# Keys and values of both layers by seven half-size products instead of eight

## The chip, the cores and the metric

The kernel runs on one core of a Trainium2 chip. The metric is the device time in microseconds of one execution, the median of several runs; lower is better. The core has a matrix engine (TensorE, PE in the profile; its weight loads are PEld), VectorE (DVE), ScalarE (ACT), GpSimd (POOL) and SyncE (SP). DMAs are issued from the SP queue and from the POOL queue.

## The reference, cut to what matters

Two layers work on 512 tokens of width 1024. Each layer is, with `mod` six vectors made from `c` by one product:

```
h = rmsnorm(x, norm1_w) * (1 + sc1) + sh1
u = h @ w_in          # pool 256, conv 3 x 256, q 512, k 512, v 512, gates 3 x 1024
q, k: RMS norm over each head of 64, partial rotary;  o = block-sparse causal attention(q, k, v)
merged = sig(g0)*(y_pool @ p_pool) + sig(g1)*(y_conv @ p_conv) + sig(g2)*(o @ p_attn)
x = x + g1 * (merged @ w_out)
h2 = rmsnorm(x, norm2_w) * (1 + sc2) + sh2
x = x + g2 * ((silu(h2 @ w_gate) * (h2 @ w_up)) @ w_down)
```

## The kernel before, in words

All activations stand with features on the 128 partitions and the 512 tokens along a row, eight tiles `k` for the width of 1024. Every product is done as three matmuls (`mm3`, L166): each operand is split into a rounded part `hi` and the rest `lo`, and hi\*hi, hi\*lo and lo\*hi are added in PSUM. One `mm3` of 512 columns adds 512 to a counter, and each 2048 columns (12 matmuls) make one **tick** (L137). A tick advances the running generators ("fibers", which hold attention's own work) and lets queued small tasks (`bulk`) be emitted, as far as a credit that grows by `bulk_rate` per tick covers their listed cost.

Weights come as a list of **chunks** of up to eight 128 x 128 blocks (`items`, L310). `next_w` (L366) hands out the next chunk and loads those up to four (later three) chunks ahead of it. A chunk is fetched by SP into a `raw` tile (three buffers, L235), its hi copy is made by ACT (L328) and its lo part by DVE (L331). Gate columns (`by_transfer`) are split without DVE: ACT makes hi (L339) and its negative (L341), and a POOL DMA adds the weights from memory to the negative (L343). There are five hi and five lo tiles, so a chunk can be split only when the chunk five before it has been used. The tag `w4` has six buffers of 4 KB per partition, `big` has 46 of 2 KB, and PSUM has four banks of tag `mm` and two pairs of tag `pair`.

A layer's first half runs in this order on PE. (1) q and three feature columns, chunk by chunk as the norm delivers tiles `k`. (2) The feature columns 6, 3 and 7 of pool and convolution. (3) `wide()` twice: keys, then values, each as four chunks of eight blocks, 4 token tiles x 8 `k` x 3 matmuls of 512 columns. After the keys, squares and sums for their norm are made (`qk_evac`, L608 to L611), and key scaling and rotary (L989, L626 to L629) are queued. After the values, ACT and DVE split them into `v` (L1003, L1004). (4) Attention starts as a fiber after three ticks, beside columns 4 and 5 with the pool product, then eight steps `j` of two gate columns and four small products into two `mm` banks each (`p1`, `p2`), then six columns of the third gate. (5) `drain()` ends attention; then eight attention products, merged with the gates (L1033, L1067, L573). (6) The output product, the second norm and the feed-forward, whose gate and up products already run as seven half-size products (`glu_pair`).

The products of `c` (`ada_dot`, L399) are made by DVE from loaded rows, one dot of 128 x 1024 per task; `pin` places an instruction behind the one traced before it on its engine. The dots of part G1 are queued beside keys and values; in layer 0 those of SC2 and SH2 are queued beside attention at a `bulk_rate` of 0.27, each dot with its own load just ahead of it (L433).

The compiler that places the instructions keeps each engine's queue in a fixed order, chosen from the program's order and from when it takes operands to be ready; buffers of one tag are handed out in the order asked for.

## Time and profile before

| | us |
|---|---|
| median of 3 runs | 1442.67 (1441.82 to 1442.86) |
| the profiled execution, its own time | 1442.24 |
| its span, first to last instruction | 1440.5 |
| PE busy | 1433.7 |
| DVE busy | 1014.5 |
| ACT busy | 714.0 |
| POOL busy | 145.7 |

The profiled execution's time is 1.7 us over its span, for what lies around it. Busy time is the union of an engine's instructions. Matmuls overlap (one is shown as 390 ns but the next starts 227 ns later), so PE's pace is read from starts, not from durations. Layer 0's stages (2), (3) and the start of (4) lie at 55.6, 72.0 and 115.5 us; layer 1's at 763.5, 781.8 and 825.4 us.

### The profile page before, as it was taken

How to read it: one execution, taken by the hardware profiler on the slowest of the kernel's cores; microseconds unless marked ns; L12 is line 12 of the kernel's file. 1: busy time of each engine (PE TensorE's matmuls, PEld its weight loads, DVE VectorE, ACT ScalarE, POOL GpSimd, SP SyncE). 2: the span in 40 equal slices, each digit the busy share in tenths (PEclk: the TensorE clock that was granted, in tenths of full speed). 3: DMA queues.
4: the chain of work that ended last, by engine and by line, in shares of the span. 5: the costliest groups of instructions: out<-in, count | busy, mean ns of one | idle time of the engine just before them, and what ended most of it. 6: DMA issues, size and time to landing. Idle time of an engine off the chain costs nothing.

```text
span 1440.5 us, 21954 instructions
## 1 busy us (share of the span) xinstructions
PE 1433.7 (100%) x8346; PEld 1261.7 (88%) x8346; DVE 1014.5 (70%) x1858; ACT 714.0 (50%) x1199; POOL 145.7 (10%) x204
## 2 busy tenths in 40 slices
PE   9999999999999999999999999999999999999999
PEld 7888888888988998999988888888889989999997
DVE  8887777649686867677798766654578747657663
ACT  5645666733653452535444466666336625525450
POOL 0000110101100311210000000011020102111200
PEclk9999999999999999999999999999999999999999
DMA  9647876665347766756536565567372537637532
GB/s 351 216 149 209 220 184 168 181 229 163 90 140 223 187 179 206 190 146 198 189 125 207 177 146 135 135 154 194 129 208 85 136 114 180 173 105 187 136 88 85
DMA packets 91049, 241.83 MB, mean 168 GB/s; under 512 B 11576, under 2 KB 24256, under 8 KB 90944
## 3 DMA queue, kind: packets, MB, share of 16 engines
q1 hardware_dynamic: 67312, 177.37, 36.8%
q0 software_dynamic: 23040, 62.93, 22.3%
q8 instruction: 65, 1.06, 0.3%
q14 instruction: 40, 0.33, 0.1%
q10 hardware_dynamic: 592, 0.14, 0.0%
HBM read 238.30 MB, written 2.10 MB: 167 GB/s over the span
## 4 chain that ended last, share of the span: by engine, by line
PE 96%; issue 1%; DMA 1%; DVE 1%; ACT 0%; ACTq 0%; DVEq 0%; POOLq 0%
PE mm L151 83%; PE pair L151 12%; PE mm L157 1%; DMA wlo<-in_ws 1%; DMA colt<-in_cols 0%; DVE big L788 0%; DVE big L795 0%; DVE big L562 0%; ACT whi L339 0%; DVE w L399 0%; ACT big L1028 0%; DVE wlo L331 0%; ACT big L575 0%; DVE tmp L555 0%; ACT big L559 0%
## 5 line engine op out<-in xcount | busy, mean ns | idle before, releaser
L151 PE MATMUL mm<-big,whi 128*128 128x512 f32 (+1 forms) x4350 | 1078.0, 339 | 1.0 <-ACT big L1028 1.0
L151 PEld LDWEIGHTS mm<-big,whi 128*128 128x128 f32 x4350 | 744.3, 190 | 87.8 <-issue 2.6
L151 PE MATMUL mm<-big,wlo 128*128 128x512 f32 (+1 forms) x2175 | 735.3, 338 | 0.1
L151 PEld LDWEIGHTS mm<-big,wlo 128*128 128x128 f32 x2175 | 412.6, 190 | 45.3 <-DMA wlo<-in_ws 0.5
L328 ACT ACTIVATE whi<-raw 128x1024 fp32r<-128x1024 f32 (+2 forms) x192 | 198.2, 1034 | 223.2 <-PE mm L151 116.8
L331 DVE TENSOR_TENSOR wlo<-raw,whi 128x1024 fp32r<-128x1024 f32 (+2 forms) x192 | 225.8, 1187 | 53.1 <-ACT whi L328 52.6
L328 ACT ACTIVATE whi<-w 128x1024 fp32r<-128x1024 f32 x72 | 76.2, 1058 | 139.5 <-PE mm L151 85.8
L1073 DVE SCALAR_TENSOR_TENSOR x<-mm,mod,x 128x512 f32<-128x512 f32 (+1 forms) x89 | 61.6, 694 | 75.2 <-PE mm L151 75.0
L399 DVE SCALAR_TENSOR_TENSOR w<-w,csil 128x1024 f32<-128x1024 f32 x80 | 95.9, 1221 | 17.8 <-DMA w<-in_ada 17.7
L331 DVE TENSOR_TENSOR wlo<-w,whi 128x1024 fp32r<-128x1024 f32 x72 | 86.8, 1221 | 28.8 <-ACT whi L328 28.1
L257 POOL DMA_DIRECT2D w<-in_ws x72 | 47.2, 673 | 465.1 <-DVE wlo L331 214.4
L343 POOL DMA_DIRECT2D wlo<-in_ws x48 | 41.0, 855 | 438.1 <-ACT wlo L341 241.5
L259 POOL DMA_DIRECT2D w<-in_ws x72 | 63.4, 906 | 159.0 <-DMA w<-in_ws 155.3
L151 PE MATMUL pair<-whi,big 128*128 128x512 f32 x224 | 76.7, 389 | 0.0
L339 ACT ACTIVATE whi<-raw 128x1024 fp32r<-128x1024 f32 x48 | 51.0, 1063 | 49.4 <-PE mm L151 32.1
L151 PE MATMUL pair<-big,whi 128*128 128x256 f32 (+1 forms) x376 | 74.0, 294 | 0.0
L151 PEld LDWEIGHTS pair<-big,whi 128*128 128x128 f32 x376 | 60.4, 191 | 2.2
L151 PE MATMUL mm<-whi,big 128*128 128x512 f32 x160 | 56.9, 392 | 0.6 <-ACT big L559 0.4
L1033 DVE SCALAR_TENSOR_TENSOR big<-big,mm 128x512 f32<-128x512 f32 x48 | 32.8, 684 | 33.1 <-PE mm L151 31.8
L151 PE MATMUL pair<-big,wlo 128*128 128x256 f32 (+1 forms) x188 | 55.3, 294 | 0.0
L341 ACT ACTIVATE wlo<-whi 128x1024 fp32r<-128x1024 f32 x48 | 50.8, 1059 | 0.3
L151 PEld LDWEIGHTS pair<-whi,big 128*128 128x128 f32 x224 | 42.1, 188 | 8.6
(212 smaller groups left out, 1349.3 us busy)
## 6 DMA issues: line engine op xcount, KB each, us to landing
raw<-in_ws SPq DMA_DIRECT2D x146, 512.0 KB, 4.4
w<-in_ada SPq DMA_DIRECT2D x80, 512.0 KB, 5.5
w<-in_ws POOLq DMA_DIRECT2D x144, 256.0 KB, 4.7
wlo<-in_ws POOLq DMA_DIRECT2D x48, 512.0 KB, 6.8
raw<-in_ws SPq DMA_DIRECT2D x64, 256.0 KB, 4.1
raw<-in_ws SPq DMA_DIRECT2D x24, 384.0 KB, 3.6
raw<-in_ada SPq DMA_DIRECT2D x16, 512.0 KB, 4.4
raw<-in_ws SPq DMA_DIRECT2D x16, 448.0 KB, 5.5
```

The lines of the kernel that those rows point to most:

```text
L151: tc.keep_in_program_order(T.matmul(*a, **k))
L157: tc.keep_in_program_order(T.transpose(*a))
L257: nc.gpsimd.dma_start(dst, self.source(0, 1))
L259: nc.gpsimd.dma_start(dst, self.source(*other), accum_op=ALU.add)
L328: A.activation(hi[:, :n], raw[:, :n], AF.Copy)
L331: ins = V.tensor_sub(lo[:, :n], raw[:, :n], f32(hi)[:, :n])
L339: A.activation(hi[:, :n], raw[:, :n], AF.Copy)
L341: A.activation(lo[:, :n], f32(hi)[:, :n], AF.Copy, scale=-1.0)
L343: nc.gpsimd.dma_start(lo[:, i:i + m].rearrange("p b n -> p (b n)"), src, accum_op=ALU.add)
L399: return V.scalar_tensor_tensor(aw, aw, 1.0, csil, op0=ALU.mult, op1=ALU.mult, accum_out=mod[l][:, part, j:j + 1])
L1033: V.scalar_tensor_tensor(sg, sg, 1.0, branch, op0=ALU.add, op1=ALU.mult)
L1073: V.scalar_tensor_tensor(x[k][:, lo:hi], src, mod[l][:, part, k:k + 1], x[k][:, lo:hi], op0=ALU.mult, op1=ALU.add)
```

## The change

Keys and values are now one product of a 2 x 2 block matrix: tokens 0 to 255 and 256 to 511 against the two halves of the width, and the two halves of the width against keys and values. It is done by seven block products (forms) instead of eight. The sums on the activation side are made by DVE (`sums_one`, `sums_two`) from a full f32 copy `h` of the normed activations, which ACT now writes in the first norms too. The sums on the weight side are made partly by POOL DMAs that add (`summed`), partly by DVE (`tensor_add` on `x`). Each form takes two chunks, so there are fourteen chunks in place of eight, each used by 12 matmuls instead of 24. Partial results are read out of PSUM between forms by ACT and DVE. The order of forms is B21, B11, R1, -V, B22, T3, T4.

Behind keys and values come three gate columns (20, 28, 21), then columns 4 and 5, then gate 29. Attention starts after five ticks instead of three. Pool weights, both convolution chains and the second pool chain are queued after keys and values instead of before. The rotary tables of layer 0 are made within them. The G1 dots move behind `drain()`, at a rate of 1.3; SC2 and SH2 run from step `j` = 2 at 0.5, each load one dot ahead.

```diff
+KEYS = 12
+AFTER_KEYS = (20, 28, 21, 4, 5, 29)
+    class KeyValue:
+        SUBS = 14
+        def blocks(self, kk, z, cp):
+            return [("in", kk * HK + 2 * cp + i, KEYS + 4 * z + b) for i in range(2) for b in range(4)]
+        def summed(self, tile, other, cp):
+            flat = tile.rearrange("p b n -> p (b n)")
+            nc.gpsimd.dma_start(flat, self.source(0, 1, cp))
+            nc.gpsimd.dma_start(flat, self.source(other[0], other[1], cp), accum_op=ALU.add)
+        def load(self, sub):
+            form, cp = divmod(sub, 2)
+            if sub == 0:
+                self.x = [w4([P, C_BLOCKS, P]) for _ in range(2)]
+                for i in range(2):
+                    self.summed(self.x[i], (1, 1), i)
+            if form == 0:
+                return split_w(self.raw(1, 0, cp), C_BLOCKS)
+            if form == 1:
+                self.near[cp] = self.raw(0, 0, cp)
+                return split_w(self.near[cp], C_BLOCKS)
+            if form == 2:
+                w = split_w(self.x[cp], C_BLOCKS)
+                pin(V.tensor_add(self.x[cp], self.x[cp], self.near[cp]))
+                self.near[cp] = self.raw(1, 0, cp)
+                return w
+            if form == 3:
+                w = split_w(self.x[cp], C_BLOCKS)
+                pin(V.tensor_add(self.x[cp], self.x[cp], self.near[cp]))
+                self.far[cp] = rawt()
+                self.summed(self.far[cp], (0, 0), cp)
+                return w
+            if form == 4:
+                return split_w(self.x[cp], C_BLOCKS)
+            return split_w(self.far[cp] if form == 5 else self.raw(1, 1, cp), C_BLOCKS)
...
         def step(n):
+            if early and n + 1 < len(every):
+                load(n + 1)
...
-            if i == 1:
-                A.activation(self.h[k][:, lo:hi], t[:, lo:hi], AF.Identity, bias=sh)
+            A.activation(self.h[k][:, lo:hi], t[:, lo:hi], AF.Identity, bias=sh)
...
+            A.activation(self.h[k], self.t, AF.Identity, bias=mod[0][:, SH1, k:k + 1])
...
-        def wide():
...
+        def sums_one(c):
+            V.tensor_sub(t3, h2[:, BLOCK:], h1[:, BLOCK:])
+            V.tensor_sub(r1, h1[:, :BLOCK], h1[:, BLOCK:])
+            V.scalar_tensor_tensor(nv, t3, -1.0, h1[:, :BLOCK], op0=ALU.mult, op1=ALU.subtract)
+            return one, two, split_from(one)
+        def sums_two(c, one, two):
+            V.scalar_tensor_tensor(two[:, BLOCK:], one[:, BLOCK:], -1.0, norm.h[HK + c][:, :BLOCK],
+                                   op0=ALU.mult, op1=ALU.subtract)
+            return split_from(two)
+        def keys_values(qk, ss, made, tables, then):
+            def form(o, name, start):
+                for cp in range(2):
+                    w = next_w()
+                    for t in range(2):
+                        for i in range(2):
+                            c = 2 * cp + i
+                            mm3(o[t], cut(rows(name, c), slice(None), slice(t * P, (t + 1) * P)), wrow(w, 4 * i),
+                                start and c == 0, c == HK - 1, skip_group_check=not start)
+                    yield cp
+            for _ in form(e, "B21", True):
+            for _ in form(a, "B11", True):
+            for t in range(2):
+                A.activation(qk[t][:, 1], heads(a[t]), AF.Copy)
+                V.tensor_add(qk[t][:, 1], qk[t][:, 1], heads(e[t]))
+                squares(1, ss, t, qk[t][:, 1].rearrange("p h d -> p (h d)"))
+            for cp in form(c, "R1", True):
+                two[cp] = sums_two(cp, *made[cp][:2])
+            for t in range(2):
+                A.activation(last[t], c[t], AF.Copy)
+            for cp in form(a, "-V", False):
+                two[2 + cp] = sums_two(2 + cp, *made[2 + cp][:2])
+            for t in range(2):
+                A.activation(qk[2 + t][:, 1], heads(a[t]), AF.Copy)
+            tables()
+            for _ in form(c, "B22", False):
+            for t in range(2):
+                V.tensor_add(qk[2 + t][:, 1], qk[2 + t][:, 1], heads(c[t]))
+                squares(1, ss, 2 + t, qk[2 + t][:, 1].rearrange("p h d -> p (h d)"))
+            then()
+            for _ in form(a, "T3", False):
+            for t in range(2):
+                A.activation(part[t], a[t], AF.Copy)
+                V.tensor_add(last[t], last[t], part[t])
+            for cp in form(d, "T4", True):
+                if cp == 0:
+                    yield from enumerate(last, 2)
+            for t in range(2):
+                V.tensor_add(part[t], part[t], d[t])
+            yield from enumerate(part)
...
-        gains = ada_tasks(l, (G1,))
-        bulk.extend(gains[:4])
-        k_ps = wide()
...
-        v_ps = wide()
...
-        fibers.append([3, attention(l, qk, v, nrq, prq, y_attn)])
+        fibers.append([5, attention(l, qk, v, nrq, prq, y_attn)])
+        bulk.append((0.4, pool_weights))
+        for j in range(2):
+            conv_chain(j, zs[j])
+        pool_chain(1, pool1)
+        bulk_rate[0] = 1.6
+        ready = [gate() for _ in range(3)]
+        flush_bulk()
...
-        bulk_rate[0] = 0.27
+        bulk_rate[0] = 0.0
...
+        ready.append(gate())
...
-            s0, s1 = gate(), gate()
+            s0, s1 = [ready.pop(0) if ready else gate() for _ in range(2)]
+            if j == 2:
+                bulk_rate[0] = 0.5
...
                 drain()
+                late = len(bulk)
+                bulk.extendleft(reversed(ada_tasks(l, (G1,))))
+                bulk_rate[0] = 1.3
```

## Rows read from the trace of the kernel before

**Rows 1.** The page, part 1 (engine busy us, share, instructions) and part 2 (granted clock).
```profile
PE 1433.7 (100%) x8346; PEld 1261.7 (88%) x8346; DVE 1014.5 (70%) x1858; ACT 714.0 (50%) x1199; POOL 145.7 (10%) x204
...
PEclk9999999999999999999999999999999999999999
```
**Rows 2.** The page, part 4: chain that ended last, shares of the span.
```profile
PE 96%; issue 1%; DMA 1%; DVE 1%; ACT 0%; ACTq 0%; DVEq 0%; POOLq 0%
```
**Rows 3.** Waits of PE, whole span: us in total, times, longest.
```profile
PE mm L151 <- ACT big L1028: 1.0, 2, 0.5
PE mm L151 <- ACT big L559: 0.4, 1, 0.4
```
**Rows 4.** Timeline of PE in the values: start us, duration us.
```profile
100.06 0.39 PE L151 MATMUL mm<-wlo,big 128*128 128x512 f32 x1
100.29 0.39 PE L151 MATMUL mm<-whi,big 128*128 128x512 f32 x1
```
**Rows 5.** Busy us (count) by stretch: PE, PEld, DVE, ACT, POOL; clock; DMA share, GB/s.
```profile
55.60:72.00 16.40, 16.40 (x74) 13.56 (x73) 14.10 (x28) 10.12 (x15) 0.00 (x0) 1.00 0.70 236
72.00:115.50 43.50, 43.50 (x194) 36.02 (x193) 35.95 (x90) 17.78 (x26) 1.84 (x2) 1.00 0.51 169
...
781.80:825.40 43.60, 43.60 (x194) 36.08 (x193) 34.34 (x76) 17.45 (x24) 1.69 (x2) 1.00 0.53 164
...
301.70:334.40 32.70, 32.70 (x146) 27.07 (x145) 20.27 (x28) 11.39 (x15) 0.00 (x0) 1.00 0.39 138
```
**Rows 6.** DVE groups, 54 to 115.5 us: count, busy us, mean ns, idle before.
```profile
L331 DVE TENSOR_TENSOR wlo<-raw,whi 128x1024 fp32r<-128x1024 f32 x11 | 13.3, 1220 | 0.8 <-ACT whi L328 0.8
L399 DVE SCALAR_TENSOR_TENSOR w<-w,csil 128x1024 f32<-128x1024 f32 x6 | 7.2, 1218 | 0.0
...
L989 DVE TENSOR_TENSOR w<-w,rq 128x512 f32<-128x512 f32 x4 | 2.7, 684 | 0.0
L626 DVE TENSOR_TENSOR tmp<-w,rtab 128x256 f32<-128x256 f32 x4 | 1.7, 418 | 0.0
...
L628 DVE TENSOR_TENSOR w<-tmp 128x128 f32<-128x128 f32 x4 | 1.1, 284 | 0.0
...
L603 DVE SCALAR_TENSOR_TENSOR rq<-rq,rq 128x64 f32<-128x64 f32 x4 | 0.9, 226 | 0.1
...
L469 DVE SCALAR_TENSOR_TENSOR rope<-rope,ang 128x32 f32<-128x32 f32 x2 | 0.4, 194 | 0.1
```
**Rows 7.** ACT groups, 54 to 132 us, same columns.
```profile
L339 ACT ACTIVATE whi<-raw 128x1024 fp32r<-128x1024 f32 x3 | 3.2, 1060 | 7.6 <-PE pair L151 7.6
L341 ACT ACTIVATE wlo<-whi 128x1024 fp32r<-128x1024 f32 x3 | 3.2, 1057 | 0.1
...
L608 ACT ACTIVATE w<-pair 128x512 f32<-128x512 f32 x5 | 3.0, 600 | 1.6 <-PE pair L151 1.6
```
**Rows 8.** Line 343, adding POOL DMA of gate columns: issue ns min/median/max, landing.
```profile
L343 POOL DMA_DIRECT2D wlo<-in_ws x48: 835/855/987, 107.3 to 1004.2; - x48
...
DMA to landing us min/median/max: 5.2/6.8/11.3
```
**Rows 9.** The page, part 6: DMA issues, count, KB each, median us to landing.
```profile
raw<-in_ws SPq DMA_DIRECT2D x146, 512.0 KB, 4.4
```
**Rows 10.** ACT groups, 16 to 54 us: layer 0's first norm.
```profile
L559 ACT ACTIVATE big<-tmp,mod 128x512 fp32r<-128x512 f32 x8 | 5.8, 725 | 4.1 <-DVE tmp L555 4.1
```
**Rows 11.** Timeline of layer 1's first norm, second half of the tokens.
```profile
733.30 0.49 DVE L545 SCALAR_TENSOR_TENSOR big<-tmp,mod,big 128x256 fp32r<-128x256 f32 x1 [0.18 <-ACT big L544]
...
734.18 0.28 PE L151 MATMUL mm<-big,wlo 128*128 128x256 f32 x1
```
**Rows 12.** Timeline of layer 0's last attention product and its read-out.
```profile
291.27 1.11 PE L151 MATMUL mm<-w,big 128*128 128x256 f32 x8
...
294.24 0.29 DVE L745 TENSOR_TENSOR big<-tmp,big 128x128 fp32r<-128x128 f32 x1 [0.38 <-ACT big L744]
```
**Rows 13.** The page, part 5: read-out of the gated products.
```profile
L1033 DVE SCALAR_TENSOR_TENSOR big<-big,mm 128x512 f32<-128x512 f32 x48 | 32.8, 684 | 33.1 <-PE mm L151 31.8
```

More of the change, by code (lines that the diff above doesn't have):

```diff
@@ L446, in ada_tasks, with step @@
     def ada_tasks(l, parts, early=False):
-        out = []
-        for part in parts:
-            for j in range(KT):
-                out.append((1.2, lambda part=part, j=j: ada_step(l, part, j, early)))
-            out.append((0.2, lambda part=part: ada_end(l, part)))
+        every = [(part, j) for part in parts for j in range(KT)]
+        kept, out = [], []
+        load = lambda n: ada_load(l, *every[n], early, kept)
+        def step(n):
+            if early and n + 1 < len(every):
+                load(n + 1)
+            if not early:
+                load(n)
+            ada_step(l, *every[n], kept)
+        if early:
+            out.append((1.2, lambda: load(0)))
+        for n, (part, j) in enumerate(every):
+            out.append((1.2, lambda n=n: step(n)))
+            if j == KT - 1:
+                out.append((0.2, lambda part=part: ada_end(l, part)))
         return out
@@ L488, in __init__ @@
             self.lo = [bigt() for _ in range(KT)]
+            self.h = [bigt(F32) for _ in range(KT)]
         def add(self, k, lo, hi):
@@ L959, in hybrid_trunk @@
                 feature_tile(pu, next_w())
+                made = [sums_one(0), sums_one(1)]
                 uc[1] = bigt(F32)
@@ L1134, in hybrid_trunk @@
         n2 = Norm()
-        n2.h = [bigt(F32) for _ in range(KT)]
         table(AF.Abs_reciprocal_sqrt, t[:, 0:1])
```

117 lines of the change are left out of this document (77 added, 40 removed).

## The prediction

> **What bounds the kernel now.** I read the page's busy shares first, then the chain of waits, the waits of PE, and last the stretches in which the change lies. PE is busy for 1433.7 of 1440.5 us at the full granted clock in every slice [rows 1], and the chain that ended last is PE for 96% of the span [rows 2]. In the list of PE's waits the largest single one on another engine in mid-kernel is 0.5 us; the two groups shown there make 1.4 us in all [rows 3]. So PE's own matmuls set the time, and a change counts through the matmuls it removes and the waits it adds. Everything on DVE, ACT, POOL and the queues is free as long as PE finds its operands ready. What cover is left is read from the stretches: keys and values take 43.5 us in each layer, in which DVE is busy 35.95 and 34.34 us, ACT about 18, POOL under 2 [rows 5].
>
> **Matmuls.** In steady state a matmul of 512 columns starts 0.23 us after the one before [rows 4]; more exactly, keys and values are 2 products x 4 token tiles x 8 `k` x 3 = 192 matmuls in 43.5 us [rows 5], so 0.2266 us each. After the change there are 7 forms x 2 chunks x 2 token tiles x 2 blocks x 3 = 168, of the same width. That removes 24 per layer, 48 in all: 48 x 0.2266 = 10.9 us. A form is 24 matmuls, 5.44 us; a chunk lasts 12 matmuls, 2.72 us, where it lasted 5.44. The stage becomes 38.1 us. All other products keep their number of matmuls. This is the whole gain: nothing else that is removed was on PE's path.
>
> **Read-outs of PSUM between the forms.** Bank pair `a` is added into by B11, -V and T3, with a read-out between, and `c` by R1 and B22. In the order chosen, one other form (5.44 us) always lies between the end of one sum in a bank and the next matmul into it. The read-out is two ACT copies of 512, 0.60 us each [rows 7], 1.2 us. So 4.2 us are spare, and I cost these waits at nothing; if ACT stood still for over 4.2 us ahead of a copy, the rest would be PE's wait. Most likely to do that is a hi copy queued ahead of it that waits for one of the two summed `far` tiles: these are a plain load (4.4 us [rows 9]) and an added one (5.2 to 11.3 [rows 8]), begun when a raw tile is free, some 6 to 10 us into the stage, and so landing at 16 to 26 us, against 27.2 and 29.9 us when T3 uses them. With hi and lo made in 1.06 + 1.22 us [rows 6, 7] this fits but for the slowest; I take zero, with 2 us per layer as the other end.
>
> **DVE in the stage.** I count what the stage emits per layer. Ten chunk splits at 1.22 = 12.2 and four weight-side adds of the same size = 4.9 [rows 6]. `sums_two`: four times one op of 256 and one of 512, 0.42 + 0.68 = 4.4 (durations of lines 626 and 989 [rows 6] for the same shapes). Eight adds and four reductions of 512: 12 x 0.68 = 8.2. The inverse roots: 17 small ops at 0.23 = 3.9; key scaling and rotary: 4 x (0.68 + 2 x 0.42 + 2 x 0.28) = 8.3; eight low halves of `v` at 0.42 = 3.4; in layer 0 rotary tables, 18 at 0.19 and 2 at 0.28 = 4.0 [rows 6]. Sum 49.3 us, and 3.9 for the two `sums_one` pieces that come in with the stage (each 3 x 0.42 + 0.68). That is 53 us of DVE work against 38.1 us of PE. So some 15 us must run over. What may run over: inverse roots, key scaling and rotary (12.2) are first used when attention makes its transposes, five ticks = 13.6 us behind the stage; the low halves of `v` and the adds of values (3.4 + 2.7) later still. Behind the stage stand three gate columns, 3 x 24 x 0.2266 = 16.3 us, whose splits take no DVE. What may not run over is the chunk splits, the adds on `x` and `sums_two`: everything queued up to the last chunk split is 53 - 12.2 - 6.1 = 35 us less the last two adds and reductions of keys, about 32 us, and has until its use, 35.4 us after the stage's start. In layer 1 the 4.0 us of tables are missing. So it fits, with 3 us to spare in layer 0 and 7 in layer 1. Removed beside it: four to eight G1 dots at 1.22 [rows 6], moved behind `drain()`, where DVE has 20.3 busy of 32.7 us [rows 5]; 8 x 1.3 = 10.4 us there make 30.7 of 32.7, still under PE. In the stretch of feature columns DVE is busy 14.1 of 16.4 [rows 5]; it loses one convolution chain and gains two `sums_one` pieces (3.9); its last chunks have 11 us and more of lead, so it only passes 2 us on.
>
> **Loads.** The splits run four chunks ahead; with 2.72 us chunks that is 10.9 us instead of 21.8. The first gate column can be split when the tenth chunk is done, 27.2 us into the stage: 1.06 + 1.06 us on ACT [rows 7], then the adding DMA from POOL, 5.2, 6.8 or 11.3 us at least, median, most [rows 8]. It lands at 34.7, 36.3 or 40.8 us and is needed at 38.5 (third matmul of the first gate). The next column may start 2.72 us later but is needed 5.44 us later. So a median landing costs nothing and the slowest 2.3 us; one in five or so is over 9 us by the spread from 6.8 to 11.3, an estimate. I take 0.5 us per layer, 0 to 2.3 as bounds. Weight bytes: each layer fetches 16 x 512 KB for keys and values where it fetched 8, and 8 x 512 KB of G1 rows leave the stage; so the bytes there stay the same in 38.1 instead of 43.5 us, the DMA share of 0.51 [rows 5] becomes 0.58, no bound. The last modulation dot of layer 1 must wait for a `w4` buffer until `x` is done with; nobody on PE's path waits for it.
>
> By the Trainium skill (DMA: Bandwidth & Descriptors, "Anatomy of one DMA"), a POOL DMA takes 2.0 us plus its bytes over 436 GB/s, 3.2 us for 512 KB as an estimate; by that rule no gate column is late and the 0.5 us per layer fall away. The trace disagrees: none of 48 landed under 5.2 us [rows 8]. The skill (SBUF, State Buffer, the "DVE blocks DMA" trap) also says that POOL cannot write descriptors while DVE holds the port they share, which speaks against a stage that puts eight more POOL DMAs beside a fuller DVE; it would add up to one DVE instruction, 1.2 us, to a landing, and 1 us per layer to my sum. The trace shows 835 to 987 ns for all 48 issues, DVE 83% busy beside some of them [rows 5, 8], so I leave it out.
>
> **The h copies.** ACT writes eight more tiles per first norm, 0.73 us each [rows 10], 5.8 us per layer. In layer 0 PE takes 4.76 us (21 matmuls) per tile and ACT idles 4.1 us before these very activations [rows 10], so they fit. In layer 1 the second token half is tight: its first lo is done at 733.79, and PE, which starts its next group at 734.30 (734.18 + 0.12), needs it with the third matmul, 0.45 us on [rows 11]: about 1 us to spare against two or three 0.4 to 0.5 us copies that may slip in front. I take 0.4 us for both layers, bounds 0 and 1.5.
>
> **Attention.** It starts two ticks later, and the same main work follows, so it ends two ticks nearer to the attention products. Before, the last read-out is done at 294.5 [rows 12] and the first attention product starts at 301.7 (the stretch of [rows 5] begins with it), its fourth operand used 2 us later; 9.2 us of margin less 5.4 leave 3.8. No wait. But steps `j` = 0 and 1 now follow each other without gates between: four `mm` banks in 5.44 us, beside attention's own four in the same ticks. Each is freed by a DVE op of 0.68 [rows 13]. PE waits for a bank if DVE is behind by more than about one step. Bounds: nothing, or all six ops of the two steps, 4.1 us per layer; the two bank waits the trace shows are 0.5 us each [rows 3], and I take 0.6 per layer. The faster SC2 and SH2 dots in layer 0 (0.5 for 0.27) add 0.2 dots per tick, 0.25 of 2.72 us; now loaded ahead, they hold DVE no longer than they last.
>
> **Sum.** Against the profiled execution: 1442.24 - 10.9 + 1.0 (gates) + 0.4 (norms) + 1.2 (banks) = 1433.9. The median of runs stands 0.43 above that execution, so I forecast **1434.3 us**, 0.6% faster. Its own range is 1430 (no new wait, and the 1.4 us of rows 3 gone as well) to 1438.
>
> **The rivals.** (a) *Waits eat the gain.* The gate columns land late and the banks run short in both layers: 2.3 + 4.1 = 6.4 us per layer at most, 12.8 in all, half to three quarters of it being plausible: 1439 to 1441, taken as 1440, no change to speak of. For it: lead time is halved exactly where the adding DMA begins to matter. Against: bounds at the far end of a spread, each twice. (b) *DVE becomes the bound, and the kernel is slower.* 53 us of DVE work stand in a fixed queue; if the order chosen puts rotary and the inverse roots ahead of chunk splits, or a pinned split behind an op that waits for PE or ACT, the stage lasts as long as DVE does: up to 53 - 38.1 = 15 us longer in layer 0 and 11 in layer 1. It decides from 10.9 us for both together; at two thirds, 17 us, the time is 1449. For it: DVE idles a sixth of this stretch now [rows 5], though it is never short of work for long; at that rate 53 us of work would last 64. Against: the splits are what the queue takes first, and the work that may wait comes last in program order. (c) *The change doesn't shorten PE*: if forms ran slower per matmul, as adding into an old bank might, 168 matmuls would have to take 0.259 us to undo the gain; against it, the starts of [rows 4] are 0.23 us apart in sums that run on in the same banks; 1443.
>
> **How the numbers follow.** Forecast 0.70, (a) 0.14, (b) 0.12, (c) 0.04. For this kernel 0.2%, 2.9 us, is about what a measurement can tell from no change. Faster by that (under 1439.8): all of the forecast, a little under half of (a): 0.76. Same (to 1445.5): the rest of (a), (c) and the weak end of (b): 0.14. Slower: 0.10. The range 1430 to 1441 leaves out about 2 in 10, nearly all of it above.
>
> **What would show it.** Right: 168 matmuls of 512 in keys and values, starts still 0.227 us apart, the stage 38 us; PE's list of waits a few us longer in all, none over 1.5; DVE over 90% busy through the stage and the three gate columns. Wrong: PE idle before T3 or T4 for lo parts of line 331 or for `sums_two` (b), before the first gates for line 343, or before `j` = 1 for banks freed by the gated products (a); or a stage that stays near 43 us with PE full (c).

## The result, and the profile after

The changed kernel takes 1463.6 us (median of 4 runs, 1460.4 to 1464.7) against 1442.5 of the kernel before: 1.4% slower, ratio 1.0143 (95% interval 1.0126 to 1.0161). The forecast was 1434.3. The profiled execution took 1460.42 us, the fastest of the four; its span is 1458.6. Of all runs named below one, of e16, took 2354.8 us at a granted clock of 0.558, and e16's median is that of the other five.

The page, parts 1 and 4, of the changed kernel (compare [rows 1, 2]):

```profile
PE 1431.7 (98%) x8298; PEld 1252.9 (86%) x8298; DVE 1065.5 (73%) x1942; ACT 748.5 (51%) x1254; POOL 158.4 (11%) x220
...
PE 83%; DVE 8%; DMA 4%; ACT 3%; issue 2%; SPq 0%; ACTq 0%; DVEq 0%; POOLq 0%
```

The 48 matmuls are gone (8346 to 8298), yet PE's part of the chain fell from 96% to 83%: it now waits for DVE, DMA and ACT. Its list of waits says for whom (total, times, longest; compare [rows 3]; line numbers here and below are those of each kernel's own text):

```profile
PE mm L155 <- DMA wlo<-in_ws: 4.6, 2, 3.1
PE pair L155 <- ACT w L1020: 3.0, 2, 1.9
PE pair L155 <- DVE wlo L395: 2.5, 1, 2.5
PE mm L155 <- ACT big L1157: 2.4, 4, 1.0
PE mm L155 <- DVE wlo L395: 1.5, 2, 0.9
PE mm L161 <- DVE big L1186: 1.5, 1, 1.5
PE mm L155 <- DVE big L657: 1.3, 1, 1.3
...
PE mm L155 <- ACT tmp L1016: 1.1, 1, 1.1
PE mm L161 <- DVE tmp L824: 1.1, 1, 1.1
```

Where the 18.1 us of the span went is read from the starts of PE's matmuls. "Behind" is from the end of keys and values to the first half-width matmul of the output product.

| us | keys, values 0 | behind 0 | keys, values 1 | behind 1 | span |
|---|---|---|---|---|---|
| before | 43.5 | 251.6 | 43.5 | 252.8 | 1440.5 |
| after | 48.6 | 261.8 | 39.4 | 259.0 | 1458.6 |
| forecast by the sum | 38.1 | 252.7 | 38.1 | 253.9 | |

So layer 0's stage missed by 10.5, what is behind it by 9.1, layer 1's by 1.3 and 5.1: 26.0 us of the 26.5 by which this execution missed its own forecast of 1433.9 (the median, 3.2 us slower than it, missed by 29.3). Stretches of the changed kernel (columns as in [rows 5]): layer 0's stage, the part of it up to the end of DVE's last chunk split, layer 1's stage, then two stretches behind long waits; below them DVE's group of chunk splits from raw tiles in the second stretch, with 4.2 us of idle time ahead of it. The clocks of 0.62 and 0.53 are what is called a half clock below: PE's granted clock is at 1.2 GHz for part of the stretch.

```profile
72.39:121.00 48.61, 41.59 (x169) 32.13 (x168) 42.26 (x92) 30.32 (x44) 5.28 (x7) 0.96 0.47 128
72.39:115.14 42.75, 35.73 (x149) 27.44 (x148) 36.63 (x73) 25.56 (x37) 3.69 (x5) 0.99 0.40 112
797.95:837.37 39.42, 38.37 (x169) 31.45 (x168) 33.01 (x56) 24.80 (x33) 4.55 (x6) 1.00 0.60 170
113.50:118.00 4.50, 3.93 (x10) 3.13 (x11) 4.40 (x12) 3.25 (x5) 1.28 (x2) 0.62 0.69 165
841.00:844.50 3.50, 3.44 (x9) 2.70 (x10) 3.50 (x12) 1.06 (x1) 0.31 (x1) 0.53 1.02 261
...
L395 DVE TENSOR_TENSOR wlo<-raw,whi 128x1024 fp32r<-128x1024 f32 x5 | 6.0, 1222 | 4.2 <-ACT whi L392 4.2
```

The chain in layer 0's stage. First, the timeline of DVE: all four `sums_one` stand at 71.7 to 82.4 us, and only behind them comes the chunk split (L395) of the third form, then the additions on `x` (L336, L341). Shown are the first and last op of the first `sums_one`, that split, the second L336 and the first L341:

```profile
71.68 0.42 DVE L968 TENSOR_TENSOR big<-big,big 128x256 f32<-128x256 f32 x1
...
73.47 0.69 DVE L654 TENSOR_TENSOR big<-big,big 128x512 fp32r<-128x512 f32 x1 [0.24 <-ACT big L653]
...
83.01 1.21 DVE L395 TENSOR_TENSOR wlo<-w,whi 128x1024 fp32r<-128x1024 f32 x1
...
87.62 1.22 DVE L336 TENSOR_TENSOR w<-w,raw 128x1024 f32<-128x1024 f32 x1
...
90.49 1.22 DVE L341 TENSOR_TENSOR w<-w,raw 128x1024 f32<-128x1024 f32 x1
```

Those additions give raw tiles back, at 88.8 and 91.7 us, and the `far` sums start only then, at 89.4 and 92.0 (POOL's timeline: the first two lines are plain loads, the last two add):

```profile
89.39 0.55 POOL L314 DMA_DIRECT2D raw<-in_ws  x1 [33.62 <-DMA raw<-in_ws]
92.00 0.54 POOL L314 DMA_DIRECT2D raw<-in_ws  x1 [2.06 <-DVE w L341]
93.14 0.87 POOL L315 DMA_DIRECT2D raw<-in_ws  x1 [0.59 <-DMA raw<-in_ws]
95.77 0.87 POOL L315 DMA_DIRECT2D raw<-in_ws  x1 [1.76 <-DMA raw<-in_ws]
```

ACT's queue has the hi copies of `far` (L392) ahead of the read-out of pair `a` (L1020), and stands. The second copy is put down to PE, but by the landings in the trace its added DMA landed at 103.43, 7.7 us after its issue. In ACT's timeline a hi copy of `x` that waited for an addition on `x` (behind it, at 96.17, stands the read-out L1016 of `c`, for which PE waits 1.1 us), the two copies of `far` and the read-out of `a`, then in PE's the last matmul of B22 and the first of T3:

```profile
94.68 1.06 ACT L392 ACTIVATE whi<-w 128x1024 fp32r<-128x1024 f32 x1 [1.88 <-DVE w L341]
...
100.33 1.06 ACT L392 ACTIVATE whi<-raw 128x1024 fp32r<-128x1024 f32 x1 [3.10 <-DMA raw<-in_ws]
...
103.53 1.06 ACT L392 ACTIVATE whi<-raw 128x1024 fp32r<-128x1024 f32 x1 [1.62 <-PE mm L155]
104.49 1.07 ACT L1020 ACTIVATE w<-pair 128x512 f32<-128x512 f32 x2
```

```profile
103.28 0.39 PE L155 MATMUL mm<-whi,big 128*128 128x512 f32 x1
105.61 0.50 PE L155 MATMUL pair<-whi,big 128*128 128x512 f32 x1 [1.95 <-ACT w L1020]
```

Then, in DVE's queue, layer 0's rotary tables (the last is L700) and five operations of the inverse roots (1.0 us) stand ahead of the splits for T4, which PE awaits from 111.6 us on:

```profile
112.59 0.29 DVE L700 TENSOR_TENSOR rtab<-sins,qkw 128x128 f32<-128x128 f32 x1
112.79 2.35 DVE L395 TENSOR_TENSOR wlo<-raw,whi 128x1024 fp32r<-128x1024 f32 x2
```

Layer 0's stage also starts 0.4 us later than before. That arises ahead of the first norm's copies, where ACT's squares wait for a load of `x`, and the first product starts at 16.84 us instead of 16.39:

```profile
9.00 1.30 ACT L877 ACTIVATE big<-x 128x512 f32<-128x512 f32 x2 [0.70 <-DMA x<-in_xT]
```

### The profile page after: what moved, and what is told of

It is laid out like the page before. It is cut to its first block, busy times and chain, and to the rows that moved or that the text cites. A ratio compares the mean times of both kernels' runs of the same rounds, so it can differ in the third digit from the quotient of the medians.

```text
span 1458.6 us, 22061 instructions
## 1 busy us (share of the span) xinstructions
PE 1431.7 (98%) x8298; PEld 1252.9 (86%) x8298; DVE 1065.5 (73%) x1942; ACT 748.5 (51%) x1254; POOL 158.4 (11%) x220
## 4 chain that ended last, share of the span: by engine, by line
PE 83%; DVE 8%; DMA 4%; ACT 3%; issue 2%; SPq 0%; ACTq 0%; DVEq 0%; POOLq 0%
PE mm L155 74%; PE pair L155 8%; DMA raw<-in_ws 2%; DVE wlo L395 2%; PE mm L161 1%; DVE w L463 1%; DMA wlo<-in_ws 1%; ACT whi L392 0%; ACT whi L403 0%; DVE raw L463 0%; DMA x<-in_xT 0%; DVE tmp L635 0%; DVE big L642 0%; DVE big L654 0%; ACT big L653 0%
## 5 line engine op out<-in xcount | busy, mean ns | idle before, releaser
L392 ACT ACTIVATE whi<-raw 128x1024 fp32r<-128x1024 f32 (+2 forms) x192 | 198.0, 1032 | 208.6 <-PE mm L155 112.8
L395 DVE TENSOR_TENSOR wlo<-raw,whi 128x1024 fp32r<-128x1024 f32 (+2 forms) x192 | 226.3, 1187 | 54.3 <-ACT whi L392 53.7
L392 ACT ACTIVATE whi<-w 128x1024 fp32r<-128x1024 f32 x84 | 88.8, 1057 | 151.3 <-PE mm L155 87.3
L395 DVE TENSOR_TENSOR wlo<-w,whi 128x1024 fp32r<-128x1024 f32 x84 | 101.2, 1220 | 29.3 <-ACT whi L392 28.6
L155 PE MATMUL pair<-whi,big 128*128 128x512 f32 x256 | 84.4, 395 | 3.0 <-ACT w L1020 3.0
L155 PEld LDWEIGHTS pair<-whi,big 128*128 128x128 f32 x256 | 48.9, 191 | 14.0 <-ACT w L1020 3.8
L653 ACT ACTIVATE big<-big 128x512 fp32r<-128x512 f32 x52 | 32.3, 626 | 44.9 <-DVE big L1225 16.8
L155 PE MATMUL pair<-wlo,big 128*128 128x512 f32 x128 | 50.9, 398 | 2.5 <-DVE wlo L395 2.5
## 6 DMA issues: line engine op xcount, KB each, us to landing
w<-in_ws POOLq DMA_DIRECT2D x144, 256.0 KB, 4.7
raw<-in_ws SPq DMA_DIRECT2D x64, 256.0 KB, 3.9
```

The source lines that it names most:

```text
L155: tc.keep_in_program_order(T.matmul(*a, **k))
L392: A.activation(hi[:, :n], raw[:, :n], AF.Copy)
L395: ins = V.tensor_sub(lo[:, :n], raw[:, :n], f32(hi)[:, :n])
L653: A.activation(hi, src, AF.Copy)
```

## The experiments

Theory 1: PE's waits come from the order of the fixed queues (DVE's block of `sums_one`, the tables, ACT in line behind late chunks, the gates' adding DMAs, raw tiles held by dot rows), so moves without less work mend them. Theory 2: DVE has more work there than fits, whatever its order. All verdicts are ratios to the kernel before, run on the same chip.

| run | median us | ratio, 95% interval | stage 0, behind 0, stage 1, behind 1 |
|---|---|---|---|
| e1 | 1461.1 | 1.0129 (1.0111, 1.0147) | 39.5, 262.8, 41.9, 256.3 |
| e2 | 1457.4 | 1.0103 (1.0088, 1.0118) | 43.5, 262.4, 39.2, 259.4 |
| e3 | 1466.2 | 1.0173 (1.0155, 1.0190) | 45.6, 268.8, 39.5, 258.7 |
| e4 | 1464.6 | 1.0151 (1.0136, 1.0167) | 46.9, 267.0, 39.5, 258.3 |
| e5 | 1453.6 | 1.0075 (1.0059, 1.0091) | 43.5, 259.2, 43.5, 254.1 |
| e6 | 1455.2 | 1.0086 (1.0069, 1.0102) | 48.3, 257.7, 39.0, 260.5 |
| e7 | 1453.9 | 1.0078 (1.0063, 1.0093) | 39.9, 267.5, 38.2, 258.6 |
| e8 | 1493.2 | 1.0349 (1.0334, 1.0365) | 51.7, 279.4, 40.0, 272.7 |
| e9 | 1456.0 | 1.0092 (1.0077, 1.0107) | 39.4, 265.0, 38.5, 259.5 |
| e10 | 1452.4 | 1.0065 (1.0047, 1.0084) | 38.8, 261.3, 38.3, 259.1 |
| e11 | 1452.0 | 1.0063 (1.0047, 1.0080) | 40.1, 261.7, 38.5, 259.7 |
| e12 | 1458.9 | 1.0108 (1.0087, 1.0129) | 38.3, 266.8, 38.3, 262.3 |
| e13 | 1446.5 | 1.0023 (1.0012, 1.0034) | 38.4, 258.3, 38.1, 257.7 |
| e14 | 1453.1 | 1.0074 (1.0059, 1.0089) | 46.8, 256.0, 39.9, 259.9 |
| e15 | 1455.4 | 1.0093 (1.0070, 1.0117) | 46.0, 259.4, 39.8, 257.1 |
| e16 | 1446.9 | 1.0032 (1.0019, 1.0045) | 38.5, 258.2, 38.5, 259.4 |
| e17 | 1442.5 | 0.9996 (0.9986, 1.0006) | 38.1, 257.8, 38.1, 255.2 |

The stretches are those of one execution each, and executions of one of these kernels lie 2 to 7 us apart: e3 and e4 are the changed kernel's program up to the gates, yet their stage 0 is 3.0 and 1.7 us shorter than its. Differences of that size between stretches show nothing by themselves.

**e1, all `sums_one` first**

```diff
+        made = [sums_one(c) for c in range(HK)]
         for j in range(2):
             if j == 1:
-                made = [sums_one(0), sums_one(1)]
...
-                made += [sums_one(2), sums_one(3)]
```

> Changed kernel, but all four sums_one are made before the three feature columns instead of beside the second and third, in both layers; nothing else moves. Theory 1 (the order of DVE's queue: the block of sums_one at 71.7 to 82.4 us delays the chunk splits, they hold the three raw tiles, the summed far tiles start late, ACT waits for them ahead of PSUM read-outs): the waits of PE at 83, 95, 97 and 103 us (5.3 us) and the 1.2 us before layer 1's B22 mostly go; layer 0's keys and values 48.6 -> about 44, layer 1's 39.4 -> 38.2, time 1463 -> about 1457. Theory 2 (DVE has more work here than PE, whatever its order): the same work before T4, layer 0's stage stays at 47 to 49, time 1461 to 1465.

Both theories got a half. The stage fell by 9.1 us, as theory 1 has it and more, but it starts 6.0 us later: the chunk split of the last feature column now stands behind the block, and PE waits 4.6 us for it. In layer 1 the stage became longer (41.9).

**e2, tables last**

```diff
-            tables()
             for _ in form(c, "B22", False):
                 pass
+            tables()
```

> Changed kernel, but layer 0's rotary tables (20 small DVE ops, 4 us) are made behind the lo parts of the last two chunks instead of ahead of them. Theory 1: the wait before T4 (2.6 us at 111.2) and the half clock behind it (some 1.9 us of slow matmuls) go; layer 0's stage 48.6 -> about 44.5, time 1463 -> about 1459; the earlier waits (83 to 103 us) stay as they are. Theory 2 (DVE's total work): key scaling and rotary come 4 us later and attention's first transposes, which had about 2 us to spare, wait for them instead: stage shorter, what follows as much longer, time 1462 to 1465.

Theory 1: the wait before T4 and the half clock behind it are gone, stage 0 is 5.1 us shorter, and the waits of 1.1, 0.9 and 1.9 us are still there. But the first gate, reached sooner, now waits 3.4 us for its DMA.

**e3, dots as before**

```diff
-            if early and n + 1 < len(every):
-                load(n + 1)
-            if not early:
-                load(n)
+            load(n)
...
-        bulk_rate[0] = 0.0
+        bulk_rate[0] = 0.27
```

> Changed kernel, but layer 0's SC2 and SH2 dots run as in the kernel before: rate 0.27 from the first step on, each load just ahead of its dot. Theory 1 (raw tiles: a row loaded one ahead holds one of the three raw tiles until its dot, in bursts of three; weight chunks then load late, ACT's hi copies wait for them in its queue ahead of attention's read-outs): layer 0 from the end of keys and values to the output product 261.8 -> 254 to 256, time 1463 -> about 1457. Rival (attention suffers from its later start and from steps 0 and 1 standing back to back): that stretch stays at 260 to 263, time 1462 to 1465.

A miss: 268.8. In DVE's timeline a dot now waits 4.58 us for its own row and holds up the read-out of a bank (L652), for which PE waits 3.9 us. Of the 7.0 us more behind the stage, about 3.8 stand at the first gate, which no dot touches (a wait of 3.7 us and a half clock behind it, against 1.5 us). The test changed the loading and the rate together, so it prices neither, and it says nothing of raw tiles.

```profile
225.47 1.22 DVE L463 SCALAR_TENSOR_TENSOR raw<-raw,csil 128x1024 f32<-128x1024 f32 x1 [4.58 <-DMA raw<-in_ada]
...
226.62 0.75 DVE L652 SCALAR_TENSOR_TENSOR big<-mm,colt,big 128x512 fp32r<-128x512 f32 x1
```

**e4, gate 20 split by DVE**

```diff
-        ... and blocks[0][2] >= 20
+        ... and blocks[0][2] >= 20 and blocks[0][2] != 20
```

> Changed kernel, but the first gate column behind keys and values (20) is split with DVE (one op of 1.22 us) instead of an adding DMA, in both layers. Theory 1 (the DMA lands 7 to 9 us after its issue and the split can't start before the tenth chunk is used): the waits of 1.65 us (layer 0) and 3.2 us (layer 1) and the half clock behind the latter (1.6 us) go, time 1463 -> about 1457.5. Theory 2 (DVE is as late as the DMA): the wait moves to that lo part, 1 to 3 us in each layer, time 1461 to 1465.

Theory 2 by its time, but for another reason: the new lo part is late by 0.9 us only; the next gate's adding DMA is now the late one (3.5 us in layer 0, and 1.4 in layer 1 behind 1.5 for the lo part).

**e5, the old products in the new order**

```diff
-        first_part[at_keys:at_keys] = [KeyValue(l)] + moved
+        first_part[at_keys:at_keys] = keys + moved
...
-        for t, src in keys_values(qk, ss, made, tables, turn):
+        k_ps = wide()
...
+        v_ps = wide()
```

> Everything of the change but the products themselves: keys and values are again eight block products (192 matmuls, old chunks, no sums), with the new order of gates, attention's late start, the moved chains and dots. Theory 1 (what follows keys and values suffers from the DVE, ACT and raw-tile backlog that the seven forms leave): keys and values 43.5 us as before, the stretch from there to the output product 252 to 255 in both layers as before (251.6, 252.8), time 1442 to 1448. Rival (the new order behind them costs by itself: steps 0 and 1 back to back, dots at 0.5 with rows loaded ahead, gates' DMAs early): that stretch 258 to 262 in layer 0, time 1450 to 1456.

The rival was right. The rearrangement alone costs 11.1 us in the medians; the trace, of its fastest execution, shows 7.6 behind layer 0's stage and 1.3 behind layer 1's. Against e5 the seven forms with their sums and DMAs make the kernel 10.0 us slower (1463.6 to 1453.6), where they were to make it 10.9 faster. What PE waits for in e5 (whole span) are read-outs of attention's transposes (L657), of the gated products (L1122) and of attention's last product (L824):

```profile
PE mm L155 <- DVE big L657: 2.0, 1, 2.0
PE mm L161 <- DVE big L1122: 1.4, 1, 1.4
...
PE mm L161 <- DVE tmp L824: 1.1, 1, 1.1
```

**e6, no dots in layer 0**

```diff
-            bulk.extend(ada_tasks(l, (SC2, SH2), True))
+            for part in (SC2, SH2):
+                V.memset(mod[l][:, part], 0.0)
+                ada_end(l, part)
```

> Changed kernel without layer 0's SC2 and SH2 dots (left out: those two vectors are their biases only). Theory 1 (rows loaded ahead hold raw tiles, so weight chunks load late and ACT waits for them ahead of read-outs): of layer 0's stretch behind keys and values the waits at 170, 222 and 288 to 298 us go (some 6 us): 261.8 -> about 255.5, like layer 1's 259.0 less its gate wait and half clock; time 1463 -> about 1457. Rival (banks and late start): 260 to 262, time 1461 to 1464.

8.4 us faster in the medians; behind layer 0's stage the traces differ by 4.1. This kernel leaves the dots out, their two vectors are their biases alone. PE's waits from 143 to 380 us are in the changed kernel those for L1186, L657 and L824 above (1.5, 1.3, 1.1) and two of 0.5 and 0.4; without the dots one is left:

```profile
PE mm L155 <- ACT big L1157: 1.0, 1, 1.0
```

So the dots make the late waits of layer 0. In e5 the waits stand at the same read-outs; e5 without the dots was not run. By which way the dots act, e10 was to tell.

**e7, `sums_one` spread, tables last**

```diff
+        made = [sums_one(0), sums_one(1)]
         qk = [w4([P, 2, HEADS, HD]) for _ in range(TT)]
...
                 pu = ps_mm()
+                made += [sums_one(2), sums_one(3)]
                 feature_tile(pu, next_w())
```

> Changed kernel with layer 0's tables behind the last chunk splits and two of the four sums_one ahead of the read-outs of q, in DVE's idle 3.3 us there, the other two one feature column earlier. Theory 1 (order): the waits at 94 to 104 us go too, layer 0's keys and values 43.5 -> 39 to 40 with at most 2 us of new wait in the feature columns, layer 1's 39.2 -> 38.5; the first gate then waits 3 to 4 us in each layer for its adding DMA; time 1457 -> about 1454. Theory 2 (DVE's total): what goes in keys and values comes back in the feature columns, as 4.6 us did with all four ahead; time 1456 to 1460.

Theory 1: both stages come to 39.9 and 38.2 with under 1 us of new wait in the feature columns, 9.7 us less in the median than the changed kernel. The first gates wait 4.2 and 2.8 us, as expected, each with a half clock behind.

**e8, gate lo parts by POOL**

```diff
-        A.activation(lo[:, :n], f32(hi)[:, :n], AF.Copy, scale=-1.0)
-        for i, m, src in runs(l, blocks):
-            nc.gpsimd.dma_start(lo[:, i:i + m]..., src, accum_op=ALU.add)
+        pin(nc.gpsimd.tensor_sub(lo[:, :n], raw[:, :n], f32(hi)[:, :n]))
```

> Changed kernel, but the lo part of every gate column is one subtraction on POOL in place of ACT's negative copy and an adding DMA. Theory 1 (the landing of 7 to 9 us is what the first gate waits for): with an operation of some 2 to 4 us the waits of 1.65 and 3.2 us and layer 1's half clock go, ACT loses 1.05 us per column; time 1463 -> about 1455. Rival (POOL's operation takes as long as the landing, or holds up DVE): same waits, 1460 to 1470.

The rival, and far beyond it: 30 us slower than the changed kernel. POOL's operation is short, 2.6 us (48 of them, one group), but DVE stands meanwhile: beside two of them, from 120.09 for 4.79 us, two DVE operations on 64 elements take 2.3 us each, which take 0.23 elsewhere.

```profile
L405 POOL TENSOR_TENSOR wlo<-raw,whi 128x1024 fp32r<-128x1024 f32 x48 | 123.0, 2565 | 317.5 <-ACT whi L403 268.2 <-DVE asm L775 17.9 <-DVE big L1184 17.5
```

```profile
120.31 2.30 DVE L682 SCALAR_TENSOR_TENSOR rq<-rq,rq 128x64 f32<-128x64 f32 x1
122.65 2.32 DVE L683 SCALAR_TENSOR_TENSOR rq<-rq,rq 128x64 f32<-128x64 f32 x1
```

DVE's read-out of a PSUM bank against one SBUF operand (L1184) keeps its 682 ns, also where it runs beside such a subtraction (13 of 48). The Trainium skill (SBUF — State Buffer, "SBUF: two separate sides") calls the port pair that DVE and GpSimd share an exclusive lock, held for a whole instruction, which a DVE operation with two SBUF inputs needs against a GpSimd one that reads SBUF; the trace agrees (2.3 us for two such operations, 682 ns with an operand in PSUM).

**e9, e10, e11: e7 with three more moves, alone and together**

e9 fetches gate 20 with the tenth chunk and splits it into two `w4` tiles; e10 loads the dot rows as two halves into `big` tiles; e11 has both, and starts the dots without saved credit.

```diff
+            if sub == 11:
+                w = split_w(self.far[1], C_BLOCKS)
+                made_early[self.l] = split_by_transfer(self.gate, self.l, self.after, True)
+                return w
...
+        if early:
+            aw = [bigt(F32), bigt(F32)]
+            for i in range(2):
+                nc.sync.dma_start(aw[i], ada[l, part, j][:, i * S:(i + 1) * S])
...
-                bulk_rate[0] = 0.5
+                bulk_rate[0], credit[0] = 0.4, -1.0
```

> e7_sums_spread, and the first gate column is fetched and split some 13 us earlier, into two tiles that the weight sums x have left, so that it needs no hi or lo buffer of the chunks. Theory 1 (what the gates wait for is only the 7 to 9 us landing counted from the earliest buffer): the waits of 4.3 us (layer 0) and 2.9 us (layer 1) and the half clock behind both (1.6 us each) go; the stretches behind keys and values 267.5 -> about 261.5 and 258.6 -> about 254; time 1454 -> about 1444. Rival (the next column 28 is then as late, as when column 20 went by DVE): 2 to 3.5 us of wait come back at 28, time 1449 to 1452.

> e7_sums_spread, and the rows of layer 0's SC2 and SH2 dots are loaded as two halves into free 2 KB tiles instead of a raw tile (two half dots and one addition per part in place of one dot). Theory 1 (a row loaded ahead holds one of three raw tiles; ACT's hi copies wait for late chunks ahead of attention's read-outs): the waits at 163, 216, 285 and 295 us (2.1, 4.0, 2.0 and 1.3) mostly go, 267.5 -> about 260, time 1454 -> about 1447. Rival (the dots' own time on DVE, in bursts of three): only part of it goes, 264 to 267, time 1451 to 1454.

> e7_sums_spread with the early first gate and the dot rows in tiles of their own, and the dots begin without a burst (no saved credit, rate 0.4). Theory 1 (four separate places where the waits come from, each mended by its own move): keys and values 39.5 and 38.2, the stretches behind them 253 to 255 each, time 1435 to 1439, faster than the kernel before by what the 48 matmuls are worth less some 3 to 6 us. Theory 2 (DVE has too much to do between 55 and 145 us whatever its order): the waits move on to the gates or to attention's first transposes, time 1443 or more.

e9: neither. In layer 0 the gates' DMAs are late by 0.3 us only (1.5 in layer 1), but PE then waits for the gates' own read-outs by ACT (2.0 and 0.9 us), which stand behind v splits that wait for DVE; no time is won. e10: the waits of PE from 143 to 380 us fell from 6.9 us in e7 (2.4, 1.6, 1.2, 1.1, 0.4, 0.2) to 1.7, none over 0.4:

```profile
PE mm L155 <- DVE big L1200: 0.4, 1, 0.4
PE mm L155 <- ACT big L670: 0.3, 1, 0.3
...
```

That points to the raw tiles. In the changed kernel's ACT timeline the hi copy at 220.78 waits for a chunk loaded late, and attention's read-out (L656) is queued behind it. That chunk's load is the second of the two at 211.20 in SP's timeline and goes out at 217.5, as the hi copy of the chunk before ends. Rows of `ada` were loaded at 200.89 and 210.44, and by the order of loads and dots the dot at 216.99 is that of the first: until then two of the three raw tiles held rows.

```profile
220.78 1.06 ACT L403 ACTIVATE whi<-raw 128x1024 fp32r<-128x1024 f32 x1 [1.73 <-DMA raw<-in_ws]
...
222.84 0.67 ACT L656 ACTIVATE big<-mm,colt 128x512 fp32r<-128x512 f32 x1
```

```profile
200.89 0.33 SPq L497 DMA_DIRECT2D raw<-in_ada  x1
...
210.44 0.33 SPq L497 DMA_DIRECT2D raw<-in_ada  x1
211.20 6.63 SPq L239 DMA_DIRECT2D raw<-in_ws  x2
...
216.99 1.22 DVE L463 SCALAR_TENSOR_TENSOR raw<-raw,csil 128x1024 f32<-128x1024 f32 x1
```

The median fell by 1.5 us only, less than the spread, and the two traces are of e7's slowest execution and e10's fastest; e10 also splits each dot in two. So the way is seen, and its price is not shown. e11: theory 2 (1452.0).

**e12, e13: ACT's queue ahead of the gates**

e12 is e11 with the edits below, and with the second `far` chunk split one chunk later; e13 leaves out that and e9's early column.

```diff
-        A.activation(lo[:, :n], f32(hi)[:, :n], AF.Copy, scale=-1.0)
+        A.activation(lo[:, :n], raw[:, :n], AF.Copy, scale=-1.0)
...
-        ready = [gate() for _ in range(3)]
+        ready = [gate(), gate()]
+        for t, src in last_two:
+            values(t, src)
+        ready.append(gate())
```

> e11_all_three, and ACT's queue is freed ahead of the first gates: the last two v splits (which wait 5 us for DVE's sums of part) are emitted behind two gates, the negative copy of a gate column is taken from the raw tile and not from its hi copy, and the second far chunk is split one chunk later. Theory 1 (what is left in e11 is ACT standing in line: 3.3 us of late tanh read-outs at 130 us, 2.3 us of the second gate's late DMA in layer 1, whose issue came 3 us behind the hi copy): both stretches 255 to 257, time 1452 -> 1441 to 1445. Theory 2 (DVE has 10 us and more of work left when keys and values end, and something always waits for it): the waits move to attention's first transposes and the pool and convolution products, time 1447 or more.

> e12_gate_reads_first without the early first gate column and without the later far chunk. Theory 1: the first gate again waits 3 to 4 us in each layer, shortened by the earlier negative copy to 2 to 3, and a half clock of 1.6 us behind it; nothing else waits long: both stretches 257 to 259, time 1445 to 1448, some 3 to 5 us over e12. Theory 2: the same time as e12, since DVE's backlog and not the gate's landing sets when attention can begin.

e13 is the fastest complete version, 0.23% slower than the kernel before, at the time that theory 1 gave it; but e12, with the early column and the later chunk, is 12 us slower. Its waits are for attention's first transposes and scores (DVE's rotary 2.1 us, ACT's read-out of q 3.6), where theory 2 had them; which of the two differences makes them so long was not settled.

**e14, e15: a DMA for an addition, and slower dots**

```diff
-                pin(V.tensor_add(self.x[cp], self.x[cp], self.near[cp]))
+                nc.gpsimd.dma_start(self.x[cp].rearrange("p b n -> p (b n)"), self.source(0, 0, cp), accum_op=ALU.add)
```

```diff
-                bulk_rate[0], credit[0] = 0.4, -1.0
+                bulk_rate[0], credit[0] = 0.3, -1.0
```

> e13_gate_reads_no_early, and the first addition on each weight sum x (2 of 1.22 us per layer) is done by a third adding DMA into x in place of DVE, which also gives the raw tile of the second form back at once. Theory 1 (DVE, 96% busy in the 35 us behind keys and values in e13, is what the rest waits for): 2.4 us less DVE work per layer, the waits behind keys and values shrink by 1 to 2 us per layer, time 1446.5 -> about 1443. Rival (two more DMAs of 512 KB, 7 to 9 us from issue to landing, come too late for the fourth form or slow the far sums): keys and values 38.4 -> 40 to 42, time 1448 to 1452.

> e14_first_add_by_dma with the SC2 and SH2 dots at a rate of 0.3 in place of 0.4. Theory 1 (each dot takes 1.36 us out of DVE's chain of one attention unit): the waits of 0.4 to 0.7 us at 154 to 161 and 260 us lessen, up to 1.5 us less than e14. Rival: the dots then run on into the attention products, beside G1's eight, and DVE is late there: same as e14 or up to 2 us more.

e14: the rival. ACT's hi copy of `x` waits for the DMA, and the read-out behind it (L1018) makes PE wait 6.6 us in layer 0's stage; behind it 2.3 us are won, as theory 1 had it, but none in layer 1. e15: the rival too: waits of 2.2 us at 344 to 348 us, where dots and G1 meet. The wait of e14:

```profile
PE pair L155 <- ACT w L1018: 6.6, 1, 6.6
```

**e16, e17: order or amount**

e16 puts e13's two v splits behind three gates; e17 is e13 without the shifted terms of the convolutions and without the doubling steps of the second pool chain.

```diff
-        ready = [gate(), gate()]
+        ready = [gate() for _ in range(3)]
...
-        ready.append(gate())
```

```diff
-                for shift, w in ((1, C_CW + 2), (2, C_CW)):
-                    V.scalar_tensor_tensor(...)
...
-            for shift in ((1, 2) if j == 0 else (1, 2, 4, 8)):
+            for shift in ((1, 2) if j == 0 else ()):
```

> e13_gate_reads_no_early with the last two v splits behind three gates in place of two, so that ACT's read-outs of attention's first transposes don't stand behind them. Theory 1 (ACT's fixed queue: in e13's layer 1 the first scores wait 1.9 us, plus 0.6 of smaller waits, for a read-out queued behind four copies that wait for DVE): that goes, layer 0 keeps its 2.3 us gate wait, time 1446.5 -> 1443.5 to 1444.5, no longer told from the kernel before. Rival (DVE's backlog: the first score waits as long for the lo part that DVE makes): 1446 to 1448.

> e13_gate_reads_no_early without 6.4 us of DVE work per layer that stands behind keys and values: the shifted terms of both convolution chains (4 ops of 0.74 us) and the four doubling steps of the second pool chain (3.5 us) are left out. Theory 2 (what is left in e13 is DVE's amount of work behind keys and values, 33.1 us busy in 34.6): the waits at 843 and 870 us in layer 1 (3.2) and 154 to 161 in layer 0 (1.7) mostly go, time 1446.5 -> 1442 to 1443. Rival (what is left is the gates' landing and ACT's order): 1445 to 1448 as before.

e16: the rival, no gain. e17, which leaves those terms out of its result: theory 2, 4.0 us in the medians. The 34.6 to 35 us behind the two stages, columns as above; first e13, then e17, last the kernel before:

```profile
110.40:145.00 34.60, 32.43 (x160) 26.12 (x159) 33.14 (x89) 23.36 (x42) 3.87 (x6) 1.00 0.84 211
822.00:857.00 35.00, 32.73 (x160) 26.15 (x159) 31.78 (x79) 22.68 (x40) 3.96 (x6) 1.00 0.70 189
```

```profile
109.90:144.50 34.60, 33.22 (x163) 26.53 (x162) 28.05 (x77) 23.71 (x44) 3.90 (x6) 1.00 0.86 217
822.00:857.00 35.00, 34.38 (x171) 27.63 (x170) 27.11 (x71) 24.80 (x46) 4.00 (x6) 1.00 0.78 203
```

```profile
115.45:150.00 34.55, 34.55 (x176) 28.32 (x175) 26.09 (x61) 19.42 (x34) 3.40 (x4) 1.00 0.72 205
825.40:860.00 34.60, 34.60 (x176) 28.33 (x175) 24.21 (x62) 21.80 (x42) 3.41 (x4) 1.00 0.68 166
```

DVE's number, the third, is the point: 26 and 24 us before, 33 and 32 in e13, where it is busy for 91 to 96%, 28 and 27 in e17. But e17's stages last 38.1 us, 10.8 less than before for the two together, and it is still no faster than the kernel before: behind them it takes 6.2 and 2.4 us more. In layer 0 that is the first gate's DMA (1.2 us), waits at 153 to 161 us for the steps' banks and for attention (0.8, 0.4, 0.3, 0.2), and two of 0.3 at 260 us. What of it the later start of attention and the changed order make by themselves was not tested.

## Why the prediction was wrong, step by step

- *Matmuls*: right. 168 per stage at 0.2266 us; e17's stages are 38.10 us, the forecast's figure.
- *Read-outs between the forms at nothing*: wrong, its other end came and more. In layer 0 PE waits 1.1 us for `c` and 1.95 for `a`, in layer 1 1.05 for `a`. For `a` it went as the text named: ACT blocked by a hi copy of a `far` tile; for `c` it was a hi copy of `x`, behind DVE's addition. The sums began 17 to 20 us into the stage, not 6 to 10.
- *DVE "fits, with 3 us to spare in layer 0"*: the step that failed first. The text put about 32 us of work, the tables among it, ahead of the end of the last chunk split, due 35.4 us after the stage's start. In the trace that end comes at 42.75: DVE is busy for 36.6 us and idle for 6.1. The work was 4.6 us short, above all because all four `sums_one` lie in the stage and not two. The idle time the sum put at nothing, as if DVE always had its operands; it waits for ACT's hi copies, these for the `far` DMAs, and these for raw tiles that DVE's own queue gives back. That was the second half of rival (b)'s condition (a split behind what waits), given 0.12. Stage 0 missed by 10.5 us; by one trace each, e2 gives back 5.1 of it by the tables' place alone, e7 8.7 by both moves.
- *What runs over has room behind*: wrong in kind. The work that runs over fills DVE there (e13), and ACT's queue stands behind it; 6.4 us less of DVE's work per layer there were worth 4.0 us (e17).
- *Attention and the moved order*: costed at 0.6 us per layer; e5, which has of the change only that order and the h copies, is 11.1 us slower than the kernel before. *The dots "hold DVE no longer than they last"* is a part of that, and in none of the rivals: without the dots the changed kernel is 8.4 us faster (e6), forecast nothing. A row loaded one ahead holds one of three raw tiles, two at times; how much of the 8.4 that makes is not shown.
- *Gates, 0.5 us per layer*: landings were as forecast (5.2, 7.1, 10.5 us least, median, most; the text's 34.7, 36.3 and 40.8 should read 0.2 less by its own terms), but the copies ahead of them come late, in layer 0 the negative one 3.0 us behind the hi copy: waits of 1.5 and 3.1 us, the second beyond the bound of 2.3, and in layer 1 the half clock.
- *The h copies*: too dear in layer 0. The 0.4 us of later start there arise before the first of them, and from the first product to keys and values both kernels take 55.6 us. In layer 1 the way there is 0.3 us longer; forecast 0.4 for both, up to 1.5.
- *Rival (a)* was also there; its price for banks was not reached. The rivals were taken as alternatives, one of three or four; here (a), (b) and the dots came together, because one late queue feeds the next.

What stays open: how the 11.1 us of e5 divide between the dots and the rest of the new order, what the raw tiles alone cost, e12, and why executions of the changed kernel lie 4 us apart and those before 1 us.

## What to carry to other kernels

An operation that is cheap on a free engine is not free in a fixed queue: for each engine write down the new queue in order, and ask of every entry what it may wait for and which PSUM read-out stands behind it. Buffers are a resource like time: a load moved ahead, or a tile kept for a later sum, takes a slot from the stream that feeds the bound engine. And where a change trades matmuls for vector work, sum that work over the stretches behind too: here DVE was busy for 33 of the next 35 us where it had been for 26, and with 6.4 us less of it the kernel was 4.0 us faster. Price a new order by itself, too: here it cost as much as the matmuls were to give.

## What the runs showed of the hardware

- Behind waits of PE of 2.45 and 3.07 us the granted clock fell to half (0.62 and 0.53 over the stretches shown, matmuls 0.427 us apart, the 1.2 GHz level), for eight to nine matmuls, some 1.6 us more each time; behind the waits of up to 1.95 us in the same execution it stayed at 2.4 GHz. In e6 it fell, for as many matmuls, behind two waits of 1.1 and 0.9 us, 1.4 us apart, behind which it stayed up in the changed kernel and in e2, and in e13 it stayed up behind a wait of 2.2 us; so the length of the last wait alone does not tell.
- POOL's subtraction of 128 x 1024 takes 2.6 us, and beside it DVE operations within SBUF that take 0.23 us took 2.3 (e8); in place of ACT's negative copies and the adding DMAs, 48 of them cost 30 us.
